# Projections of a hybrid decoder layer: one plain float32 matmul per weight block in place of three float32r passes

## Chip, core and metric

One core of one Trainium2 chip runs the program. The metric is the device time of one execution in microseconds (us), a median over runs. The core has TensorE (PE, whose weight loads are shown apart as PEld), VectorE (DVE), ScalarE (ACT), GpSimd (POOL) and SyncE (SP, which here only issues DMAs).

## What is computed

One inference step of one decoder layer on 320 tokens: 256 of a prompt and 8 sequences of 8 new tokens. Three residual parts follow each other, each behind an RMSNorm, all in float32:

```python
u, z, xbc, dt_raw, g_pool, g_ssm = jnp.split(h @ w_in, IN_SPLITS, axis=-1)
pooled, pool_new = _pool_mixer(u, pool_prev, pos, w_pool_group, pool_scale)
...
merged = jax.nn.sigmoid(g_pool) * (pooled @ w_pool_out) + jax.nn.sigmoid(g_ssm) * (y @ w_ssm_out)
x = x + merged @ w_out                                  # mixer: pooling and state-space branch
x = x + _cross_attn(_rmsnorm(x), mem_k, mem_v, w_q, w_o)  # 4 heads, 256 memory tokens
x = x + (jax.nn.silu(g) * v) @ w_down                   # g, v: causal conv of _rmsnorm(x) @ w_up
```

D_MODEL is 2048, the state-space branch is 4096 wide with 64 heads in 8 groups, the FFN is 5632 wide. The memory's keys and values (256 tokens by 2048) are projections too. Nearly all the arithmetic is such products of activations with weights that are read once.

## The kernel before

Activations lie with features on the partitions: 16 chunks of 128 features by 320 tokens. A projection (`dense`, line 92; `dense2`, line 104) makes a chunk of 128 outputs in a PSUM tile `acc` by adding up blocks: a block is 128 by 128 weights against 128 by 320 activations. The weights come in units of 128 by 1024 float32, 0.5 MB, eight blocks (`unit`, line 68), 785 in all.

A product is not one matmul. `unit` loads the unit into `raw` (line 73, SP's queue), casts it to float32r on ACT (`wh`, line 76) and has DVE subtract that from `raw` (`wl`, line 77): a high and a low part. The activations are split in the same way (`split`, line 120, and `split_gain`, line 124, with a gain in it): ACT makes the high part, DVE the low one (`a0h` and `a0l`, `a1h` and `a1l`, and so on). `mm3` (line 80) then issues three float32r matmuls per block: high by high (line 82), high weights by low activations (line 83), low weights by high activations (line 84). The memory's values have the tokens as the stationary side and 512 columns of weights as the moving one, three passes again (lines 229 to 231). The memory's keys go through `dense` with 256 tokens.

`raw` has 4 buffers, `wh` and `wl` 3 each. A scheduler orders each engine's instructions by priority, and `unit` runs at a priority AHEAD = 300 steps earlier than where it stands in the code, so that the loads and splits are queued ahead of the blocks that use them. SP's queue works in order: a load that waits for a buffer holds up what stands behind it, which also holds the loads of the states, of cached keys and values, of x and of constants.

The stages: `mem_and_norm` (line 198: memory values, the first norm, memory keys; `by_token` loads x and takes the memory's norm to tokens by two transposes of `rm`, line 288), `time_steps`, then eight groups of the state-space branch, whose scan (`ssd`, with `update`, line 611, the state updates by line 623) is woven between the projections; then the pooling branch, the output projection, cross-attention and the FFN. Some small products were plain float32 matmuls already: the sum of squares against ones in `rstd` (line 156), the attention's scores (line 882) and values (line 921), and the scan's products. `rstd` ends in a Newton step on DVE (lines 161 to 164), whose tile `newton` shares the tag `sq` and its two buffers with the squares of `square_into` (line 146).

Of the kernel before, what the change touches and what calls it, by code (L numbers as in the profile page):

```python
# [11 lines left out]
F32 = mybir.dt.float32  # L12
# [7 lines left out]
D = 2048  # L20
# [15 lines left out]
AHEAD = 300  # L36
SLABS = [(0, 12), (12, 12), (24, 12), (36, 8)]

# columns of the array of per-feature vectors
# [9 lines left out]
# columns of the array of constants  # L49
# [8 lines left out]
class Kernel:  # L58
# [9 lines left out]
    def unit(self, src):  # L68
        """Loads a [128, 1024] block of weights and splits it into high and low parts."""
        nc = self.nc  # L70
        with self.tc.high_priority(offset=self.ahead):
            raw = self.wraw.tile([128, 1024], F32, tag="raw", name="raw")
            nc.sync.dma_start(out=raw, in_=src)
            wh = self.wsp.tile([128, 1024], F32R, tag="wh", name="wh")
            wl = self.wsp.tile([128, 1024], F32R, tag="wl", name="wl")
            nc.scalar.copy(out=wh, in_=raw)  # L76
            nc.vector.tensor_tensor(out=wl, in0=raw, in1=wh.bitcast(F32), op=ALU.subtract)  # L77
        return wh, wl

    def mm3(self, out, wh, wl, xh, xl, first, last):  # L80
        nc = self.nc
# [10 lines left out]
    def dense(self, w, n, xh, xl, kc=KC, cols=128, t=T):  # L92
        """One chunk of outputs from kc chunks of inputs: a PSUM tile [cols, t]."""
        out = self.acc(t)[:cols]
        per = 1024 // cols
        for u in range((kc + per - 1) // per):
            wh, wl = self.unit(w[n, u] if cols == 128 else w)
            for j in range(min(per, kc - u * per)):
                k = u * per + j
                s = slice(j * cols, (j + 1) * cols)  # L100
                self.mm3(out, wh[:, s], wl[:, s], xh[:, k, :], xl[:, k, :], k == 0, k == kc - 1)
        return out

    def dense2(self, w, n2, k4s, xh, xl, k0=0):
        """Two chunks of outputs, units of two by four chunks: w[n2, u] holds [2, 4, 128]."""
        a = [self.acc(), self.acc()]
        for ui, u in enumerate(k4s):
            wh, wl = self.unit(w[n2, u])
            for o in range(2):
                for j in range(4):  # L110
                    s = slice((o * 4 + j) * 128, (o * 4 + j + 1) * 128)
                    k = k0 + ui * 4 + j
                    self.mm3(a[o], wh[:, s], wl[:, s], xh[:, k, :], xl[:, k, :],
                             ui == 0 and j == 0, ui == len(k4s) - 1 and j == 3)
        return a
# [4 lines left out]
    def split(self, hi, lo, src):  # L120
        self.nc.scalar.copy(out=hi, in_=src)  # L121
        self.nc.vector.tensor_tensor(out=lo, in0=src, in1=hi.bitcast(F32), op=ALU.subtract)  # L122
# [17 lines left out]
    def square_into(self, ssum, src, first, n):  # L140
        """Adds the squares of src to ssum."""
# [8 lines left out]
    def rstd(self, out, ssum, ones, n, more=()):  # L150
        """1 / sqrt(mean + eps) on all partitions, from sums of squares per partition."""
# [7 lines left out]
        # one Newton step: r * (1.5 - 0.5 * (mean + eps) * r * r)  # L159
# [32 lines left out]
    def acts0(self):  # L192
        return [self.a0.tile([128, KC, T], F32R, tag=t, name=t) for t in ("a0h", "a0l")]

    def acts1(self):
        return [self.a1.tile([128, KC, T], F32R, tag=t, name=t) for t in ("a1h", "a1l")]

    def mem_and_norm(self, p):
        """Keys and values of the memory; the first norm. Returns the jobs that remain."""
# [3 lines left out]
        self.xnh, self.xnl = self.acts0()  # L203
# [7 lines left out]
        mgh = p.tile([128, KC, MEM], F32R, name="mgh")  # L211
        mgl = p.tile([128, KC, MEM], F32R, name="mgl")
# [6 lines left out]
        def values(cb, before=lambda u: None):  # L219
            a = [self.acc(512), self.acc(512)]  # L220
            for u in range(8):
                before(u)
                wh, wl = self.unit(I["w_mem_v"][cb, u])
                for j in range(2):
                    k = 2 * u + j
                    s = slice(j * 512, j * 512 + 512)
                    for mc in range(2):
                        ms = slice(mc * 128, mc * 128 + 128)
                        nc.tensor.matmul(a[mc], lhsT=mgh[:, k, ms], rhs=wh[:, s], start=k == 0, stop=False)
                        nc.tensor.matmul(a[mc], lhsT=mgh[:, k, ms], rhs=wl[:, s], start=False, stop=False)  # L230
                        nc.tensor.matmul(a[mc], lhsT=mgl[:, k, ms], rhs=wh[:, s], start=False, stop=k == KC - 1)
# [10 lines left out]
        def norm_x():  # L242
            self.rstd(rx, sx, self.ones_d, T)
            for k in range(KC):
                xn = p.tile([128, T], F32, tag="xn", name="xn", bufs=2)
                nc.vector.scalar_tensor_tensor(out=xn, in0=x[:, k, :], scalar=self.vec(V_MIX + k), in1=rx,
                                               op0=ALU.mult, op1=ALU.mult)
                self.split(self.xnh[:, k, :], self.xnl[:, k, :], xn)
# [3 lines left out]
        def keys(n):  # L252
# [3 lines left out]
            a = self.dense(I["w_mem_k"], n, mgh, mgl, t=MEM)  # L256
# [5 lines left out]
        def split_mem(u):  # L262
# [4 lines left out]
            for k in (2 * u, 2 * u + 1):  # L267
                self.split_gain(mgh[:, k, :], mgl[:, k, :], m[:, k, :], self.gain_mkv[:, k:k + 1])
# [32 lines left out]
    def time_steps(self, s, p):  # L301
        """dt and the cumulated decays of all heads; their tables by token and by feature."""
# [9 lines left out]
        if True:  # L312
# [7 lines left out]
            a = self.dense(I["w_dt"], 0, self.xnh, self.xnl, cols=64)  # L320
# [5 lines left out]
            # log(1 + u) = 2 atanh(u / (2 + u))  # L326
# [85 lines left out]
    def xbc(self, s, g):  # L412
        """Projection, conv and SiLU of a group's B, C and x, features on partitions: six jobs."""
# [3 lines left out]
        def job(i):  # L417
# [8 lines left out]
            a = self.dense(I["w_xbc"], 6 * g + i, self.xnh, self.xnl)  # L426
# [24 lines left out]
    def ssd(self, s, g, r):  # L451
        """The scan of a group, in parts that go between other products."""
# [8 lines left out]
        def by_token():  # L461
# [12 lines left out]
            # B by token  # L474
# [5 lines left out]
            # C B, causal  # L480
# [10 lines left out]
            # decays between tokens, times C B  # L491
# [41 lines left out]
        def quads(q):  # L533
            """x and B of four batches by token, as high and low parts: rows [h l h l] and [h h l l]."""
# [77 lines left out]
        def update(i):  # L612
            """The states of two batches: rows of x against the batch's rows of B."""
# [32 lines left out]
    def gate(self, s, g, v, c):  # L646
        """y * silu(z) for one chunk."""
# [4 lines left out]
        a = self.dense(self.I["w_z"], 4 * g + c, self.xnh, self.xnl)  # L652
# [5 lines left out]
    def group_norm(self, s, g, v):  # L658
        """RMSNorm over the group, split."""
# [3 lines left out]
        yh = s.tile([128, 4, T], F32R, tag="yh", name="yh")  # L663
        yl = s.tile([128, 4, T], F32R, tag="yl", name="yl")
        for c in range(4):
            nc.vector.scalar_tensor_tensor(out=y[:, c], in0=y[:, c], scalar=self.vec(V_SN + 4 * g + c), in1=r,
                                           op0=ALU.mult, op1=ALU.mult)
            self.split(yh[:, c], yl[:, c], y[:, c])
        v["yhl"] = (yh, yl)

    def ssm_out(self, g, v, n2):
        nc = self.nc
        for o, a in enumerate(self.dense2(self.I["w_ssm_out"], n2, [g], *v["yhl"])):
# [6 lines left out]
    def gate_pool(self, s, c):  # L680
        """sigmoid of a chunk of the pooling branch's gates, kept in DRAM."""
        nc = self.nc
        a = self.dense(self.I["w_gp"], c, self.xnh, self.xnl)
# [4 lines left out]
    def mixer_ssd(self):  # L688
        self.gp_dram = self.dram.tile([128, KC, T], F32, name="gp_dram")
        with ExitStack() as st:  # L690
# [17 lines left out]
            for g in range(GROUPS):  # L708
# [8 lines left out]
                if prev is None:  # L717
                    # no earlier group to project: the same steps over fewer jobs
# [17 lines left out]
    def mixer_pool(self):  # L736
        nc, I, O = self.nc, self.I, self.O
        ph, pl = self.acts1()
        with ExitStack() as st:
# [8 lines left out]
            def window(k):  # L748
                dh = s.tile([128, 4, T], F32R, tag="dh", name="dh")
                dl = s.tile([128, 4, T], F32R, tag="dl", name="dl")  # L750
                w = 2 << k
                for i in range(4):
                    c = 4 * k + i
                    a = self.dense(I["w_u"], c, self.xnh, self.xnl)
# [14 lines left out]
                    df = s.tile([128, T], F32, tag="df", name="df", bufs=2)  # L769
# [5 lines left out]
                    self.split(dh[:, i], dl[:, i], df)  # L775
                return dh, dl

            def mix(k, d):
                for n2 in range(2):
                    for o, a in enumerate(self.dense2(I["w_pool_group"][k], n2, [0], *d)):  # L780
                        c = 4 * k + 2 * n2 + o
                        self.split_gain(ph[:, c], pl[:, c], a, self.vec(V_PS + c))
# [6 lines left out]
            for c in range(KC):  # L789
                a = self.dense(I["w_gs"], c, self.xnh, self.xnl)  # L790
# [8 lines left out]
            mh, ml = self.acts0()  # L799
# [420 lines left out]
```

## Time and profile before

| | us |
|---|---|
| median of 3 runs | 2975.48 (2974.54 to 2977.37) |
| profiled execution, span | 2977.2 |
| PE busy | 2930.6 (98%), 20082 instructions |
| PEld busy | 2841.3 (95%) |
| DVE busy | 1745.7 (59%) |
| ACT busy | 1311.4 (44%) |
| POOL busy | 512.6 (17%) |

Matmuls overlap in the profile: the duration of one runs from its start to the modelled end of its last output, so what a matmul costs in a stream is the distance from its start to the next start, not its duration. In a merged timeline row of n equal records that distance is the row's length less the last record's duration, by n - 1. Idle time of an engine is given with what ended it.

### The profile page before, as it was taken

The numbers are of one execution on the slowest core, as the hardware profiler recorded it, in microseconds if no ns is written. First come the engines' busy times: TensorE is split into PE (matmuls) and PEld (weight loads), VectorE is DVE, ScalarE is ACT, GpSimd is POOL, SyncE is SP. The second block draws the span as 40 slices with busy tenths as digits, with TensorE's granted clock in tenths as the row PEclk, the third lists the DMA queues.
The fourth block names the chain that finished last, engine by engine and source line by source line (L and its number), as shares of the span: only waits on it lengthen the run. The fifth ranks groups of instructions, "written<-read, shape, count | busy, mean of one in ns | idle before, by whom it ended". The sixth has DMA issues, their size and how long they took to land.

```text
span 2977.2 us, 49666 instructions
## 1 busy us (share of the span) xinstructions
PE 2930.6 (98%) x20082; PEld 2841.3 (95%) x20082; DVE 1745.7 (59%) x2442; ACT 1311.4 (44%) x1908; POOL 512.6 (17%) x624
## 2 busy tenths in 40 slices
PE   8999999999999999999999999999999999999997
PEld 6999899999999999999999998799999999999997
DVE  5667667677687565553355543356666646645644
ACT  6545555545545444443333433344444424433434
POOL 4014333243243220321111100010000000000002
PEclk9999999999999999999999999999999999999998
DMA  8775564555555645554556558744444444444443
GB/s 284 233 235 170 184 207 152 191 191 163 197 184 163 202 159 170 180 166 152 162 171 211 171 191 285 280 145 148 149 155 150 156 152 150 151 152 149 152 152 110
DMA packets 170150, 530.34 MB, mean 178 GB/s; under 512 B 20928, under 2 KB 47808, under 8 KB 165696
## 3 DMA queue, kind: packets, MB, share of 16 engines
q1 hardware_dynamic: 155360, 493.39, 51.1%
q10 hardware_dynamic: 14560, 33.78, 3.1%
q8 instruction: 157, 2.57, 0.4%
q14 instruction: 73, 0.60, 0.1%
HBM read 491.85 MB, written 35.25 MB: 177 GB/s over the span
## 4 chain that ended last, share of the span: by engine, by line
PE 86%; DMA 2%; DVE 1%; POOL 1%; issue 0%; ACT 0%; DVEq 0%; SPq 0%; ACTq 0%; POOLq 0%
PE acc L82 27%; PE acc L83 27%; PE acc L84 27%; DMA g<-la_dram 1%; PE misc L190 1%; DMA vc<-in_cache_v_dram 1%; PE misc L574 1%; DMA kc<-in_cache_k_dram 1%; PE misc L597 1%; PE misc L623 1%; PE misc L882 0%; PE misc L921 0%; PE misc L930 0%; DVE wl L77 0%; POOL g L495 0%
## 5 line engine op out<-in xcount | busy, mean ns | idle before, releaser
L77 DVE TENSOR_TENSOR wl<-raw,wh 128x1024 fp32r<-128x1024 f32 x785 | 1001.5, 1276 | 841.9 <-ACT wh L76 838.0
L76 ACT CAST wh<-raw 128x1024 fp32r<-128x1024 f32 x785 | 821.0, 1047 | 1235.4 <-PE acc L83 843.4
L82 PE MATMUL acc<-a0h,wh 128*128 128x320 f32 (+1 forms) x2960 | 922.1, 312 | 0.7 <-ACT a0h L121 0.7
L83 PE MATMUL acc<-a0l,wh 128*128 128x320 f32 (+1 forms) x2960 | 914.9, 309 | 0.4 <-DVE a0l L122 0.4
L84 PE MATMUL acc<-a0h,wl 128*128 128x320 f32 (+1 forms) x2960 | 914.8, 309 | 0.0
L82 PE MATMUL acc<-a1h,wh 128*128 128x320 f32 x1920 | 594.9, 310 | 0.0
L84 PE MATMUL acc<-a1h,wl 128*128 128x320 f32 x1920 | 593.4, 309 | 0.0
L83 PE MATMUL acc<-a1l,wh 128*128 128x320 f32 x1920 | 593.2, 309 | 0.0
L82 PEld LDWEIGHTS acc<-a0h,wh 128*128 128x128 f32 (+1 forms) x2960 | 555.8, 188 | 8.4 <-issue 3.6
L83 PEld LDWEIGHTS acc<-a0l,wh 128*128 128x128 f32 (+1 forms) x2960 | 556.1, 188 | 5.5 <-issue 3.2
L84 PEld LDWEIGHTS acc<-a0h,wl 128*128 128x128 f32 (+1 forms) x2960 | 555.9, 188 | 2.3 <-issue 2.1
L82 PEld LDWEIGHTS acc<-a1h,wh 128*128 128x128 f32 x1920 | 360.9, 188 | 6.0 <-issue 5.4
L83 PEld LDWEIGHTS acc<-a1l,wh 128*128 128x128 f32 x1920 | 361.0, 188 | 0.2
L84 PEld LDWEIGHTS acc<-a1h,wl 128*128 128x128 f32 x1920 | 360.9, 188 | 0.0
L82 PE MATMUL acc<-yh,wh 128*128 128x320 f32 x512 | 162.4, 317 | 0.0
L83 PE MATMUL acc<-yl,wh 128*128 128x320 f32 x512 | 159.7, 312 | 0.0
L84 PE MATMUL acc<-yh,wl 128*128 128x320 f32 x512 | 159.7, 312 | 0.0
L148 POOL TENSOR_TENSOR ssum<-ssum,sq 128x320 f32<-128x320 f32 x63 | 63.4, 1007 | 506.4 <-ACT sq L147 506.3
L1026 POOL COPY fnew<-fext 128x18 f32<-128x18 f32 x88 | 18.4, 209 | 546.1 <-DVE fext L1025 546.1
L438 DVE SCALAR_TENSOR_TENSOR ca<-ext,vecs,ca 128x344 f32<-128x344 f32 x144 | 99.2, 689 | 11.3 <-ACT ca L436 10.3
L82 PEld LDWEIGHTS acc<-yh,wh 128*128 128x128 f32 x512 | 97.7, 191 | 6.8 <-ACT sb L621 4.2
L1031 DVE SCALAR_TENSOR_TENSOR fca<-fext,vecs,fca 128x336 f32<-128x336 f32 x176 | 99.6, 566 | 3.1
(279 smaller groups left out, 3353.7 us busy)
## 6 DMA issues: line engine op xcount, KB each, us to landing
raw<-in_w_up_dram SPq DMA_DIRECT2D x176, 512.0 KB, 3.5
raw<-in_w_xbc_dram SPq DMA_DIRECT2D x96, 512.0 KB, 3.7
raw<-in_w_down_dram SPq DMA_DIRECT2D x88, 512.0 KB, 3.5
raw<-in_w_z_dram SPq DMA_DIRECT2D x64, 512.0 KB, 4.3
raw<-in_w_ssm_out_dram SPq DMA_DIRECT2D x64, 512.0 KB, 3.6
raw<-in_w_mem_v_dram SPq DMA_DIRECT2D x32, 512.0 KB, 4.9
raw<-in_w_mem_k_dram SPq DMA_DIRECT2D x32, 512.0 KB, 4.2
hin<-in_state_ssm_dram SPq DMA_DIRECT2D x32, 512.0 KB, 4.3
```

Of the source, the lines that this page charges most:

```text
L76: nc.scalar.copy(out=wh, in_=raw)
L77: nc.vector.tensor_tensor(out=wl, in0=raw, in1=wh.bitcast(F32), op=ALU.subtract)
L82: nc.tensor.matmul(out, lhsT=wh, rhs=xh, start=first, stop=False)
L83: nc.tensor.matmul(out, lhsT=wh, rhs=xl, start=False, stop=False)
L84: nc.tensor.matmul(out, lhsT=wl, rhs=xh, start=False, stop=last)
L148: nc.gpsimd.tensor_tensor(out=ssum, in0=ssum, in1=sq, op=ALU.add)
L190: self.nc.tensor.transpose(out, src, self.ident[:n, :n])
L438: nc.vector.scalar_tensor_tensor(out=ca[:, 0:344], in0=e[:, j:j + 344], scalar=self.vec(V_CW + 48 * j + c), in1=ca[:, 0:344], op0=ALU.mult ...
L574: nc.tensor.matmul(ps[64 * hh:64 * hh + 64, j * 128:j * 128 + n], lhsT=xd[j][:, h * 64:h * 64 + 64], rhs=gt[j][:, h, :n], start=True, stop ...
L597: nc.tensor.matmul(pq[32 * j:32 * j + 32, :], lhsT=Ct[:, SEQ + 8 * b:SEQ + 8 * b + 32], rhs=v["hin"][b // 2][:, b % 2, :], start=True, sto ...
L623: nc.tensor.matmul(ps, lhsT=sb, rhs=xr, start=True, stop=True)
L1031: nc.vector.scalar_tensor_tensor(out=ca[:, :336], in0=e[:, j:j + 336], scalar=self.vec(V_FW + 88 * j + c), in1=ca[:, :336], op0=ALU.mult, ...
```

## The change

Each projection block becomes one matmul with float32 operands. `unit` only loads; `split`, `split_gain` and `mm3` go; activations are kept once, in float32, written by the instruction that made them (or by `gained`, ACT alone). `raw` has 16 buffers and the pool of `wh` and `wl` is gone. The state-space branch's `y` gets two buffers, since the projection now reads it and not its split.

```diff
+WBUFS = 16
...
     def unit(self, src):
         with self.tc.high_priority(offset=self.ahead):
             raw = self.wraw.tile([128, 1024], F32, tag="raw", name="raw")
-            nc.sync.dma_start(out=raw, in_=src)
-            wh = self.wsp.tile([128, 1024], F32R, tag="wh", name="wh")
-            wl = self.wsp.tile([128, 1024], F32R, tag="wl", name="wl")
-            nc.scalar.copy(out=wh, in_=raw)
-            nc.vector.tensor_tensor(out=wl, in0=raw, in1=wh.bitcast(F32), op=ALU.subtract)
-        return wh, wl
+            self.nc.sync.dma_start(out=raw, in_=src)
+        return raw
-    def mm3(self, out, wh, wl, xh, xl, first, last):
-        nc.tensor.matmul(out, lhsT=wh, rhs=xh, start=first, stop=False)
-        nc.tensor.matmul(out, lhsT=wh, rhs=xl, start=False, stop=False)
-        nc.tensor.matmul(out, lhsT=wl, rhs=xh, start=False, stop=last)
+    def mm(self, out, w, x, first, last):
+        self.nc.tensor.matmul(out, lhsT=w, rhs=x, start=first, stop=last)
...
-    def split_gain(self, hi, lo, src, g):
-        self.nc.scalar.activation(out=hi, in_=src, func=AF.Copy, scale=g)
-        self.nc.vector.scalar_tensor_tensor(out=lo, in0=src, scalar=g, in1=hi.bitcast(F32),
-                                            op0=ALU.mult, op1=ALU.subtract)
+    def gained(self, out, src, g):
+        self.nc.scalar.activation(out=out, in_=src, func=AF.Copy, scale=g)
...
-        self.wraw = self.pool("wraw", 4)
-        self.wsp = self.pool("wsp", 3)
+        self.wraw = self.pool("wraw", WBUFS)
...
     def acts0(self):
-        return [self.a0.tile([128, KC, T], F32R, tag=t, name=t) for t in ("a0h", "a0l")]
+        return self.a0.tile([128, KC, T], F32, tag="a0", name="a0")
...
-            y = v["y"] = s.tile([128, 4, T], F32, tag="y", name="y")
+            y = v["y"] = s.tile([128, 4, T], F32, tag="y", name="y", bufs=2)
...
-                        self.split(oh[:, 4 * h + dc, :SEQ], ol[:, 4 * h + dc, :SEQ], ps)
+                        (nc.scalar.copy if dc % 2 else nc.vector.tensor_copy)(out=o_[:, 4 * h + dc, :SEQ], in_=ps)
```

The code loses its comments too, so line numbers move: line 82 to 84 become line 77, line 156 becomes 141, 190 becomes 174, 623 becomes 602, 586 becomes 565, 882 becomes 854.

On PE at the start of the program (memory values; `ssm` is the memory's sum of squares, `rm` its norm, `sx` the sum of squares of x), before, around the two transposes of `rm`:

```order
L229 MATMUL acc<-wh,mgh 128x512
L230 MATMUL acc<-wl,mgh 128x512
L231 MATMUL acc<-wh,mgl 128x512
L190 MATMUL misc<-cst,rm 128x128 x2
L229 MATMUL acc<-wh,mgh 128x512
```

and now, from the first matmul on:

```order
L77 MATMUL acc<-raw,mg 128x512 x36
L141 MATMUL misc<-ssm,ones_d 128x256
L77 MATMUL acc<-raw,mg 128x512 x27
L174 MATMUL misc<-cst,rm 128x128 x2
L77 MATMUL acc<-raw,mg 128x512 x33
L141 MATMUL misc<-sx,ones_d 128x320
L77 MATMUL acc<-raw,mg 128x512 x32
L77 MATMUL acc<-mg,raw 128x256 x128
```

The three passes have become one matmul, and the transposes stand behind 63 of them.

On SP's queue in the same place (`m` is the memory, `x_in` the input x), before:

```order
L266 DMA m<-in_mem_dram 128x1024
L73 DMA raw<-in_w_mem_v_dram 128x1024 x6
L274 DMA cst<-in_cst_dram 128x388
L73 DMA raw<-in_w_mem_v_dram 128x1024
L275 DMA vecs<-in_vecs_dram 128x752
L73 DMA raw<-in_w_mem_v_dram 128x1024
L277 DMA x_in<-in_x_dram 128x1280
```

and now:

```order
L245 DMA m<-in_mem_dram 128x1024
L73 DMA raw<-in_w_mem_v_dram 128x1024 x22
L253 DMA cst<-in_cst_dram 128x388
L254 DMA vecs<-in_vecs_dram 128x752
L73 DMA raw<-in_w_mem_v_dram 128x1024
L256 DMA x_in<-in_x_dram 128x1280
```

Six weight loads stand ahead of both pieces, so the first part of x is behind 14 loads before and behind 29 now.

On DVE in the first group of the state-space branch (`g` and `gs_` are the decays, `yo` the off-diagonal part, `hin` a state), before:

```order
L496 TENSOR_SCALAR g<-g 128x1024
L77 TENSOR_TENSOR wl<-raw,wh 128x1024
L496 TENSOR_SCALAR g<-g 128x1024
L586 TENSOR_TENSOR yo<-misc,el 128x4x128
L77 TENSOR_TENSOR wl<-raw,wh 128x1024
L608 TENSOR_TENSOR yo<-misc,el 128x4x32
```

and now:

```order
L475 TENSOR_SCALAR g<-g 128x1024 x2
L475 TENSOR_SCALAR gs__991<-gs__991 64x512
L565 TENSOR_TENSOR yo<-misc,el 128x4x128
L417 SCALAR_TENSOR_TENSOR ca<-ext_986,vecs,ca 128x344
L587 TENSOR_TENSOR yo<-misc,el 128x4x32
```

The weight splits are gone from between the steps, and the third minimum stands ahead of the first `yo`.

## Rows read from the trace of the kernel before

**Rows 1.** The page: busy time, granted clock, DMA total, chain by engine.
```profile
PE 2930.6 (98%) x20082; PEld 2841.3 (95%) x20082; DVE 1745.7 (59%) x2442; ACT 1311.4 (44%) x1908; POOL 512.6 (17%) x624
PEclk9999999999999999999999999999999999999998
DMA packets 170150, 530.34 MB, mean 178 GB/s; under 512 B 20928, under 2 KB 47808, under 8 KB 165696
...
PE 86%; DMA 2%; DVE 1%; POOL 1%; issue 0%; ACT 0%; DVEq 0%; SPq 0%; ACTq 0%; POOLq 0%
```

**Rows 2.** The page's groups, weight splits: count | busy us, mean ns | idle before, releaser.
```profile
L77 DVE TENSOR_TENSOR wl<-raw,wh 128x1024 fp32r<-128x1024 f32 x785 | 1001.5, 1276 | 841.9 <-ACT wh L76 838.0
L76 ACT CAST wh<-raw 128x1024 fp32r<-128x1024 f32 x785 | 821.0, 1047 | 1235.4 <-PE acc L83 843.4
```

**Rows 3.** Busy by stretch: length, PE, PEld, DVE, ACT, POOL (records), clock, DMA, GB/s.
```profile
2100.00:2400.00 300.00, 300.00 (x2047) 300.00 (x2046) 188.65 (x308) 126.32 (x164) 19.27 (x78) 1.00 0.48 154
```

**Rows 4.** Scores: timeline of PE (start, length), and the line's records (ns min/median/max).
```profile
1759.61 3.18 PE L882 MATMUL misc<-kt,qt 128*128 128x256 f32 x14
...
L882 PE MATMUL misc<-kt,qt x64: 378/379/382, 1759.6 to 1899.9; 128*128 128x256 f32 x64
```

**Rows 5.** Sum of squares against ones: timeline of PE, and the line's records.
```profile
344.96 0.70 PE L156 MATMUL misc<-ssum,ones_g 128*128 128x320 f32 x2
...
L156 PE MATMUL misc<-ssum,ones_g x16: 431/432/432, 345.0 to 1152.3; 128*128 128x320 f32 x16
```

**Rows 6.** Block counts: line 82 over the span (PE, PEld), keys, values by form.
```profile
0.00:2977.20 2977.20, 1870.37 (x6032) 1134.62 (x6032) 0.99 0.55 178
...
L82 PE MATMUL acc<-mgh,wh 128*128 128x256 f32 x256 | 72.4, 283 | 0.0
...
L229 PE MATMUL acc<-wh,mgh 128*128 128x512 f32 x128 | 52.3, 410 | 8.1 <-ACT wh L76 7.3 <-ACT v L237 0.8
```

**Rows 7.** Busy by stretch, in the memory's keys.
```profile
180.00:200.00 20.00, 20.00 (x169) 20.00 (x168) 11.83 (x20) 8.15 (x10) 0.98 (x4) 1.00 0.75 261
```

**Rows 8.** Timeline of PE in the memory's values: first and fifteenth of a run.
```profile
99.66 0.39 PE L231 MATMUL acc<-wh,mgl 128*128 128x512 f32 x1
...
102.94 0.39 PE L230 MATMUL acc<-wl,mgh 128*128 128x512 f32 x1
```

**Rows 9.** Waits of PE: who waited for whom, us in total, times, longest.
```profile
PE misc L623 <- DVE yo L586: 10.9, 6, 3.8
PE acc L229 <- ACT wh L76: 7.3, 1, 7.3
PE misc L623 <- ACT sb L621: 4.0, 1, 4.0
```

**Rows 10.** Timelines of DVE and of PE behind PE's longest interior stall.
```profile
300.86 1.51 DVE L496 TENSOR_SCALAR g<-g 128x1024 f32<-128x1024 f32 x1 [2.62 <-POOL g L495]
...
302.89 1.21 DVE L77 TENSOR_TENSOR wl<-raw,wh 128x1024 fp32r<-128x1024 f32 x1
...
306.68 0.47 PE L82 MATMUL acc<-a0h,wh 128*128 128x320 f32 x1
306.95 0.47 PE L83 MATMUL acc<-a0l,wh 128*128 128x320 f32 x1
```

**Rows 11.** The start: two stretches, x's first square, the norm's end, early passes.
```profile
0.00:60.00 60.00, 51.81 (x207) 40.21 (x208) 37.05 (x40) 42.47 (x74) 30.50 (x35) 1.00 0.77 269
60.00:80.00 20.00, 19.88 (x86) 15.67 (x85) 9.90 (x9) 9.20 (x12) 3.34 (x2) 1.00 0.94 325
...
L144 ACT ACTIVATE sx<-x_in x1: 455/455/455, 40.4 to 40.4; 128x320 f32<-128x320 f32 x1
...
L164 DVE TENSOR_TENSOR rm<-rm,newton x1: 426/426/426, 45.6 to 45.6; 128x256 f32<-128x256 f32 x1
...
10.84 0.63 PE L230 MATMUL acc<-wl,mgh 128*128 128x512 f32 x1
11.26 0.63 PE L231 MATMUL acc<-wh,mgl 128*128 128x512 f32 x1
```

More of the change, by code (lines that the diff above doesn't have):

```diff
@@ L90, in misc, with dense @@
         return self.psm.tile([128, 512], F32, tag="misc", name="misc")
-    def dense(self, w, n, xh, xl, kc=KC, cols=128, t=T):
+    def dense(self, w, n, x, kc=KC, cols=128, t=T):
         out = self.acc(t)[:cols]
@@ L192, in acts0 @@
     def acts0(self):
-        return [self.a0.tile([128, KC, T], F32R, tag=t, name=t) for t in ("a0h", "a0l")]
+        return self.a0.tile([128, KC, T], F32, tag="a0", name="a0")
     def acts1(self):
-        return [self.a1.tile([128, KC, T], F32R, tag=t, name=t) for t in ("a1h", "a1l")]
+        return self.a1.tile([128, KC, T], F32, tag="a1", name="a1")
     def mem_and_norm(self, p):
@@ L228, in values @@
                         ms = slice(mc * 128, mc * 128 + 128)
-                        nc.tensor.matmul(a[mc], lhsT=mgh[:, k, ms], rhs=wh[:, s], start=k == 0, stop=False)
-                        nc.tensor.matmul(a[mc], lhsT=mgh[:, k, ms], rhs=wl[:, s], start=False, stop=False)
-                        nc.tensor.matmul(a[mc], lhsT=mgl[:, k, ms], rhs=wh[:, s], start=False, stop=k == KC - 1)
+                        self.mm(a[mc], mg[:, k, ms], wt[:, s], k == 0, k == KC - 1)
             return a
@@ L244, in norm_x @@
             for k in range(KC):
-                xn = p.tile([128, T], F32, tag="xn", name="xn", bufs=2)
-                nc.vector.scalar_tensor_tensor(out=xn, in0=x[:, k, :], scalar=self.vec(V_MIX + k), in1=rx,
+                nc.vector.scalar_tensor_tensor(out=self.xn[:, k, :], in0=x[:, k, :], scalar=self.vec(V_MIX + k), in1=rx,
                                                op0=ALU.mult, op1=ALU.mult)
-                self.split(self.xnh[:, k, :], self.xnl[:, k, :], xn)
         kts = {}
@@ L425, in job @@
                 nc.gpsimd.memset(r["C"][:, T:], 0.0)
-            a = self.dense(I["w_xbc"], 6 * g + i, self.xnh, self.xnl)
+            a = self.dense(I["w_xbc"], 6 * g + i, self.xn)
             e = self.ext[self.ei % 3]
@@ L651, in gate @@
         y = v["y"]
-        a = self.dense(self.I["w_z"], 4 * g + c, self.xnh, self.xnl)
+        a = self.dense(self.I["w_z"], 4 * g + c, self.xn)
         z = s.tile([128, T], F32, tag="z", name="z", bufs=1)
@@ L667, in group_norm @@
                                            op0=ALU.mult, op1=ALU.mult)
-            self.split(yh[:, c], yl[:, c], y[:, c])
-        v["yhl"] = (yh, yl)
     def ssm_out(self, g, v, n2):
         nc = self.nc
-        for o, a in enumerate(self.dense2(self.I["w_ssm_out"], n2, [g], *v["yhl"])):
+        for o, a in enumerate(self.dense2(self.I["w_ssm_out"], n2, [g], v["y"])):
             dst = self.accs[:, 2 * n2 + o]
@@ L682, in gate_pool @@
         nc = self.nc
-        a = self.dense(self.I["w_gp"], c, self.xnh, self.xnl)
+        a = self.dense(self.I["w_gp"], c, self.xn)
         t = s.tile([128, T], F32, tag="z", name="gp", bufs=1)
@@ L748, in window @@
             def window(k):
-                dh = s.tile([128, 4, T], F32R, tag="dh", name="dh")
-                dl = s.tile([128, 4, T], F32R, tag="dl", name="dl")
+                d_ = s.tile([128, 4, T], F32, tag="d_", name="d_", bufs=2)
                 w = 2 << k
@@ L753, in window @@
                     c = 4 * k + i
-                    a = self.dense(I["w_u"], c, self.xnh, self.xnl)
+                    a = self.dense(I["w_u"], c, self.xn)
                     e = exts[c % 2]
@@ L774, in window @@
                                                    scalar=1.0 / w, in1=es[:, :, 15:], op0=ALU.mult, op1=ALU.subtract)
[L775 to L776 removed]
+                return d_
             def mix(k, d):
                 for n2 in range(2):
[L780 removed]
+                    for o, a in enumerate(self.dense2(I["w_pool_group"][k], n2, [0], d)):
                         c = 4 * k + 2 * n2 + o
[L782 removed]
+                        self.gained(ph[:, c], a, self.vec(V_PS + c))
             d = window(3)
@@ L789, in mixer_pool @@
             for c in range(KC):
-                a = self.dense(I["w_gs"], c, self.xnh, self.xnl)
+                a = self.dense(I["w_gs"], c, self.xn)
                 t = s.tile([128, T], F32, tag="z", name="gs", bufs=1)
@@ L803, in mixer_pool @@
                     nc.sync.dma_start(out=sg, in_=self.gp_dram[:, c:c + 4])
-                a = self.dense(I["w_pool_out"], c, ph, pl)
+                a = self.dense(I["w_pool_out"], c, ph)
                 t = sg[:, c % 4]
                 nc.vector.tensor_tensor(out=t, in0=t, in1=a, op=ALU.mult)
-                nc.gpsimd.tensor_tensor(out=t, in0=t, in1=self.accs[:, c], op=ALU.add)
-                self.split(mh[:, c], ml[:, c], t)
-        return mh, ml
+                nc.gpsimd.tensor_tensor(out=m[:, c], in0=t, in1=self.accs[:, c], op=ALU.add)
+        return m
     def residual(self, c, a, gain, hl):
@@ L815, in residual, with mixer_out @@
         if gain is not None:
-            self.split_gain(hl[0][:, c], hl[1][:, c], self.x[:, c], self.vec(gain + c))
+            self.gained(hl[:, c], self.x[:, c], self.vec(gain + c))
         self.sum_square(c, self.x[:, c])
-    def mixer_out(self, mh, ml):
+    def mixer_out(self, m):
         nc, I = self.nc, self.I
@@ L826, in mixer_out @@
         for c in range(KC):
-            self.residual(c, self.dense(I["w_out"], c, mh, ml), V_MQ, hl)
+            self.residual(c, self.dense(I["w_out"], c, m), V_MQ, hl)
         return hl
@@ L833, in next_rstd, with attention @@
         return r
-    def attention(self, xh, xl):
+    def attention(self, xg):
         nc, I, O = self.nc, self.I, self.O
         sc = 1.0 / math.sqrt(HD)
-        oh, ol = self.acts0()
+        o_ = self.acts0()
         with ExitStack() as st:
@@ L940, in values_out @@
                     cs = slice(SEQ + 32 * q, SEQ + 32 * q + 32)
-                    self.split(oh[:, 4 * h:4 * h + 4, cs].rearrange("p c (b t) -> p c b t", b=4),
-                               ol[:, 4 * h:4 * h + 4, cs].rearrange("p c (b t) -> p c b t", b=4), src)
+                    nc.vector.tensor_copy(out=o_[:, 4 * h:4 * h + 4, cs].rearrange("p c (b t) -> p c b t", b=4), in_=src)
                 return [
@@ L1008, in up @@
                 else:
-                    hl = [s.tile([128, 12, T], F32R, tag=t, name=t) for t in ("fh", "fl")]
+                    hl = s.tile([128, 12, T], F32, tag="fh", name="fh")
                 prev = s.tile([128, 2, 12, NB, 2], F32, tag="fprev", name="fprev", bufs=1)
@@ L1016, in up @@
                         c = v * FC + i0 + i
-                        a = self.dense(I["w_up"], c, xh, xl)
+                        a = self.dense(I["w_up"], c, xg)
                         if not rxs:
@@ L1035, in up @@
                         parts.append(ca)
-                    ac = s.tile([128, T], F32, tag="ac", name="ac", bufs=2)
+                    ac = hl[:, i]
                     g_, v_ = parts
@@ L1051, in down @@
                 for c2 in range(KC // 2):
-                    for o, a in enumerate(self.dense2(I["w_down"], c2, range(i0 // 4, (i0 + n) // 4), *hl)):
+                    for o, a in enumerate(self.dense2(I["w_down"], c2, range(i0 // 4, (i0 + n) // 4), hl)):
                         c = 2 * c2 + o
@@ L1083, in run @@
             m = self.mixer_pool()
-            hl = self.mixer_out(*m)
-            hl = self.attention(*hl)
-            self.ffn(*hl)
+            hl = self.mixer_out(m)
+            hl = self.attention(hl)
+            self.ffn(hl)
             self.final()
```

56 lines of the change are left out of this document (23 added, 33 removed).

## The prediction, made before the changed kernel ran

> **What bounds the kernel now.** I read the page's first part, then the chain that ended last: PE is busy 2930.6 of 2977.2 us and has 86% of the chain, and its weight loads are 95% busy [rows 1]. A busy PE is not yet a PE at its limit, so the next view is one dense stretch. From 2100 to 2400 us (the up-projection) PE has no idle time, the clock is at 1.00, and 2047 records touch the 300 us; two of them cross its edges, so one pass starts every 300/2045 = 0.1467 us [rows 3]. A block (128 by 128 weights against 320 tokens) takes three such passes: 0.440 us. The splits that feed those passes look costly (1001.5 us on DVE, 821.0 on ACT), but the idle time in front of them is 842 and 1235 us, and most of it waits for ACT's half or for PE to free a buffer [rows 2]: both engines run behind PE, not ahead of it. DMA moves 530 MB, 178 GB/s on the mean [rows 1], where it carried 269 in the first 60 us [rows 11]; at that rate the bytes need 1970 us. So PE's passes are the bound, and the question is what a plain float32 matmul costs on PE against three passes of 0.1467 us.
>
> **The price of a plain block.** The trace has plain float32 matmuls already, in the attention and the norms. The scores of a head run just behind a dense stretch: at 1759.61 fourteen records of 256 columns take 3.18 us, the last of them 0.379, so they start (3.18 - 0.379)/13 = 0.2155 us apart [rows 4]. That is two records per matmul: four heads times 2 times 4 is 32 matmuls in the program, and the view of that line counts 64 [rows 4]. So 256 columns cost 0.431 us, at full clock, each with new weights. The other width that is there is the one needed: the sum of squares against ones, 320 columns, two records in 0.70 us with a last one of 0.432, so 0.268 apart [rows 5]; 0.2155 x 320/256 gives 0.2694. I take 0.269, 0.538 us a block (bounds 0.536 and 0.540). Three passes cost 0.440, so **each block becomes 0.098 us dearer**.
>
> **Part by part.**
> Blocks of 320 tokens: line 82 issues the first pass of each block and counts 6032, of which 256 are the memory keys', so 5776 are left [rows 6]. 5776 x 0.098 = +566 us (bounds 554 and 578). All of it lies on PE, nothing covers it.
> Memory keys, 256 blocks of 256 tokens [rows 6]: from 180 to 200 us 169 records touch 20 us, 167 starts, 0.1198 apart [rows 7]; three are 0.359, plain is 0.431, so 256 x 0.072 = +18 us.
> Memory values, 128 blocks of 512 columns [rows 6]: 14 starts from 99.66 to 102.94 us are 0.2343 apart [rows 8], three are 0.703; plain by columns is 4 x 0.2155 = 0.862; 128 x 0.159 = +20 us.
> The weight splits leave DVE and ACT (1001.5 and 821.0 us [rows 2]), and so do the splits of the activations. What PE gets from that is only idle time that it has now. Its list of waits is short: 10.9 us for DVE and 4.0 us for ACT in front of the state updates (line 623), 7.3 at the start [rows 9]; what is left is a few microseconds of loads in the attention. The one at 300 us shows the mechanism: DVE's scaling of the off-diagonal part (line 586) stands in its queue behind a minimum that waited 2.62 us for POOL, and behind that a weight split of 1.21 us stands ahead of the next step [rows 10]; the state update itself waits for those steps to free its PSUM buffer. The split goes; POOL's part stays, and in the new order the third minimum of the group stands ahead of line 586's step too, but PE gives both more time, since eight blocks last 4.3 us where they lasted 3.5. After the stall PE's passes start 0.27 apart for a while [rows 10], half the usual rate, so a stall costs more than its idle time. I take **-15 us**; bounds 0 and -30 (all of line 623's 14.9, the other interior waits, and the slow passes behind each).
> The start: PE's first matmul waits 7.3 us for the cast of the first weight block [rows 9]; without the cast -1 us (0 to -2). The number of weight buffers rises from 4 raw and 3 split to 16, and a load is put on SP's queue 300 steps early in both, which is now more blocks, as a block has fewer steps. So SP's queue runs further ahead, and what is behind 29 weight loads in it waits for PE to finish 13 blocks. The input x is there: in the order before it follows 14 loads, now 29. 29 loads of 0.52 MB, the memory tokens (2.1 MB) and constants are 18 MB, at 269 GB/s 67 us, at 325, the most that one stretch of 20 us reached [rows 11], 55 us. Who waits for x: DVE's Newton step for the memory's norm writes a buffer of the squares' tag, so it waits for POOL to add the first squares of x (the tag has two buffers), and behind it the two transposes of that norm on PE. PE comes to them after 63 plain matmuls: 6.3 + 63 x 0.862 + some 3 for its slow first microseconds (passes 0.43 apart as late as 11 us, where 0.234 is usual [rows 8, 11]) = 63 us. In the trace the norm is done 5.6 us after x's first square starts (40.4 to 46.0 [rows 11]), so it would be ready between 60 and 72: a new stall of 0 to 10 us, I take **+5**.
> Later SP loads with the same risk (states, cached keys) wait for buffers of their own that are freed many blocks before the weights behind them are needed, 16 blocks being 69 us of PE work; I cost them at nothing, and at 5 us if I am wrong. Weights are no new bound: 0.5 MB per 4.3 us is 122 GB/s. The gain on the mixer's y (two buffers instead of one plus its split) is freed DVE and ACT time off the path.
>
> **Sum**: 2977.2 + 566 + 18 + 20 - 15 - 1 + 5 = 3570 us for the profiled execution. The runs of before had a median 1.7 us under the profiled span, so 3569; I say 3570. Low end: 2977 + 554 + 37 - 30 - 2 = 3536; high end: 2977 + 578 + 39 + 10 + 5 = 3609.
>
> **Rivals.** (1) *Faster: the second record costs nothing of its own.* If a block were worth one record of 0.269, PE would lose 5776 x 0.171 = 988 us, and with DMA at 1970 us the kernel would take about 2000. The kernel is faster than before from the point where a block costs less than 0.440, that is a record under 0.22. Against it: records of 256 columns stand 0.2155 apart and those of 320 columns 0.268, in proportion to columns, and each matmul has two [rows 4, 5]; nor can the freed DVE and ACT pay, since PE is idle only 46.6 us in all [rows 1]. The Trainium skill, Perfetto Trace Analysis, section Engine Utilization, gives the array's output rate as divided by 2 for FP32_LOW_HIGH; taken as the price of a whole float32 matmul, that is this rival. The trace agrees with it for one record only (0.2155 us for 256 columns is half of 2.4 GHz), and every matmul has two of them. 2%.
> (2) *Dearer in a long stream.* The passes of today start 0.1467 apart where 320 columns at 2.4 GHz are 0.133, 10% more; the plain rows show 1% more (0.269 to 0.267). The plain ones are short runs; if hundreds in a row pay the 10% too, a block costs 0.587, and 6160 blocks add 0.05 us each: about 3870. Fourteen in a row, with new weights for each matmul, show none of it [rows 4]. 4%.
> (3) *The clock.* If a mostly plain stream were granted 1.2 GHz for part of the time, each per cent of the time costs 36 us. The fourteen plain records at 1759 us run at the full rate, right behind three-pass work; no long plain stretch is there to look at. 3%, at 3650 and above.
> (4) *The freed engines hide more than I think, or the start's stall is longer*: inside the bounds above.
> That the change doesn't do what it says is out: the order on PE has one matmul per block.
>
> **How the numbers follow.** The forecast's case has 90%, rivals 1 to 3 have 2, 4 and 3%, and 1% is left for no change. The range 3535 to 3610 is that of the forecast's own bounds; the other cases lie outside it and hold 10%. Faster by over 0.2% 2%, within 0.2% (what a measurement of this kernel can tell from no change, some 6 us) 1%, slower 97%.
>
> **What would show it.** In the profile after, a dense stretch at full clock has records 0.269 apart, 1115 in 300 us. PE's records number 20082 less 18480 passes plus 12320, 13922. DVE is busy under 750 us and ACT under 500, PE over 98%; the chain is again PE's. Around 63 us PE waits a few microseconds for the transposes of the memory's norm, and line 623's successor waits in one group at most. A spacing under 0.22 us, a spacing near 0.29, or a clock row below 9 would each make the forecast wrong, by the rival named.

## The result and the profile after

The changed kernel takes 3560.3 us (median of 4 runs, 3559.49 to 3561.03), the one before 2975.0 beside it: a ratio of 1.196, 95% interval 1.195 to 1.198. The forecast was 3570 in a range from 3535 to 3610. The profiled execution has a span of 3559.2 us against 2977.2.

From the page of the kernel after, as in [rows 1]: the busy times (share of the span, instructions), the granted clock and the total of the DMA:

```profile
PE 3528.7 (99%) x13922; PEld 2463.6 (69%) x13922; DVE 700.9 (20%) x1461; ACT 491.0 (14%) x989; POOL 393.3 (11%) x624
PEclk9999999999999999999999999999999999999999
DMA packets 170077, 529.36 MB, mean 149 GB/s; under 512 B 20928, under 2 KB 47808, under 8 KB 165696
```

DVE lost 1045 us of work and ACT 820, and PE still has almost no idle time: 30.5 us of the span, where it had 46.6. PE's records fell from 20082 to 13922, the number that two records per plain matmul make. What one of them costs is read in a stretch without idle time, as in [rows 3]. Busy time by stretch of the kernel after (length, then PE, PEld, DVE, ACT, POOL with their records, clock, DMA share, GB/s), first the start, then the up-projection:

```profile
0.00:60.00 60.00, 54.06 (x122) 24.08 (x123) 0.00 (x0) 18.28 (x41) 11.87 (x23) 1.00 0.87 321
2500.00:2800.00 300.00, 300.00 (x1116) 211.74 (x1115) 68.09 (x173) 31.35 (x52) 16.93 (x69) 1.00 0.40 125
```

1116 records touch the 300 us and two of them began before it: 300/1114 = 0.2693 us a record, 0.539 us a block, where three passes took 0.440. The weight loads are busy for 212 of the 300 us where they were busy all the time [rows 3], so it is not their rate that sets the price of a block.

PE's waits in the kernel after, which answer to [rows 9] (who waited for whom: us in total, times, longest):

```profile
PE acc L77 <- DMA raw<-in_w_mem_v_dram: 5.9, 1, 5.9
PE misc L602 <- ACT sb L600: 5.1, 6, 3.2
PE misc L876 <- DMA kc<-in_cache_k_dram: 1.7, 1, 1.7
PE misc L174 <- DVE rm L149: 0.5, 1, 0.5
```

The start is the load itself now, 5.9 us where it was load and cast, 7.3. The state updates (line 602, line 623 before) wait 5.1 us in place of 14.9. The transposes of the memory's norm (line 174) wait half a microsecond, where I had put 5 us.

### The profile page after: what moved, and what is told of

Its sections match the earlier page's. It is cut to its first block, busy times and chain, and to the rows that moved or that the text cites. A ratio compares the mean times of both kernels' runs of the same rounds, so it can differ in the third digit from the quotient of the medians.

```text
span 3559.2 us, 34307 instructions
## 1 busy us (share of the span) xinstructions
PE 3528.7 (99%) x13922; PEld 2463.6 (69%) x13922; DVE 700.9 (20%) x1461; ACT 491.0 (14%) x989; POOL 393.3 (11%) x624
## 5 line engine op out<-in xcount | busy, mean ns | idle before, releaser
L77 PE MATMUL acc<-a,raw 128*128 128x320 f32 (+1 forms) x9760 | 2647.3, 433 | 0.4 <-DVE a L913 0.4
L77 PEld LDWEIGHTS acc<-a,raw 128*128 128x128 f32 (+1 forms) x9760 | 1848.7, 190 | 781.2 <-issue 17.1
L77 PE MATMUL acc<-y,raw 128*128 128x320 f32 x1024 | 284.1, 434 | 0.0
L77 PEld LDWEIGHTS acc<-y,raw 128*128 128x128 f32 x1024 | 192.2, 190 | 81.8 <-DVE accs L653 5.0
L77 PE MATMUL acc<-fh,raw 128*128 128x320 f32 x640 | 172.6, 432 | 0.0
L1000 ACT ACTIVATE fca<-fext,vecs 128x336 f32<-128x336 f32 x88 | 58.7, 667 | 820.2 <-DVE fext L997 820.2
L77 PEld LDWEIGHTS acc<-fh,raw 128*128 128x128 f32 x640 | 121.6, 190 | 50.7
L77 PE MATMUL acc<-raw,mg 128*128 128x512 f32 x256 | 113.0, 602 | 5.9 <-DMA raw<-in_w_mem_v_dram 5.9
L77 PE MATMUL acc<-mg,raw 128*128 128x256 f32 x512 | 110.9, 379 | 0.0
L77 PEld LDWEIGHTS acc<-mg,raw 128*128 128x128 f32 x512 | 97.2, 190 | 14.1 <-issue 1.0
L594 POOL TENSOR_TENSOR hin<-hin,dec 128x1024 f32<-128x1024 f32 x32 | 63.5, 2005 | 77.3 <-PE misc L576 77.3
```

Source lines behind the costliest of these rows:

```text
L77: self.nc.tensor.matmul(out, lhsT=w, rhs=x, start=first, stop=last)
L594: nc.gpsimd.tensor_tensor(out=t.rearrange("p b (h d) -> p b h d", h=8), in0=t.rearrange("p b (h d) -> p b h d", h=8), in1=bcast(self.dec[: ...
L1000: nc.scalar.activation(out=ca[:, :336], in_=e[:, :336], func=AF.Identity, scale=self.vec(V_FW + c), bias=self.vec(V_FB + c))
```

## The experiments

Each is timed beside the kernel before on its own chip. That had a median of 2979.4 us for the runs in the FFN alone, without the low part, with 4 buffers and with two passes, and of 2980.2 for the three others.

**One part alone: plain blocks in the FFN.** The kernel before, with the projections of the FFN as plain blocks of float32 weights and activations, and all others in three passes.

```diff
-                        a = self.dense(I["w_up"], c, xh, xl)
+                        a = self.dense_plain(I["w_up"], c, xf)
...
-                    for o, a in enumerate(self.dense2(I["w_down"], c2, range(i0 // 4, (i0 + n) // 4), *hl)):
+                    for o, a in enumerate(self.dense2_plain(I["w_down"], c2, range(i0 // 4, (i0 + n) // 4), hl)):
```

> The kernel before with plain float32 blocks in the FFN alone (176 + 88 units, 2112 blocks), its weights and activations not split, 4 raw buffers as before. If each block is dearer by 0.098 us wherever it stands, +207 us: 3182 us (3170 to 3190). If the loss of the whole change comes from something that grows with the whole program (queue order, buffers, clock), clearly less or more than 207.

Measured: 3185.6 us, ratio 1.0695 (1.0679 to 1.0711), 206 us over the kernel before beside it. 206/2112 = 0.0976 us a block, and 0.098 was the estimate. Its dense stretch, in the FFN:

```profile
2500.00:2800.00 300.00, 300.00 (x1116) 211.77 (x1115) 54.66 (x135) 21.79 (x36) 11.83 (x48) 1.00 0.39 124
```

The same 1116 records as in the kernel after. The loss comes with the blocks and needs nothing of the change outside the FFN: 2112 of the 6160 blocks are 34%, and 206 of 585 us are 35%.

**The splits without the passes.** The kernel before, where DVE no longer makes the weights' low part; the third pass takes the high part a second time.

```diff
-            wl = self.wsp.tile([128, 1024], F32R, tag="wl", name="wl")
...
-            nc.vector.tensor_tensor(out=wl, in0=raw, in1=wh.bitcast(F32), op=ALU.subtract)
-        return wh, wl
+        return wh, wh
```

> The kernel before, without DVE's low part of the weights: the third pass of each block uses the high part again, so one correction term is missing from the products. PE's work is the same, DVE loses some 1000 us. If PE's passes are the bound, only idle time in front of PE can go: about 2960 us (2945 to 2977), PE at 0.1467 us a pass in dense stretches. If the weight splits hold PE up in a way that its idle time doesn't show, the kernel gains 100 us or more.

Measured: 2976.7 us (10 runs), ratio 0.9991 (0.998 to 1.0001): no change that this measurement can tell. The page, and PE's waits for line 621, which is line 623 of the kernel before:

```profile
PE 2929.8 (98%) x20082; PEld 2842.2 (95%) x20082; DVE 778.6 (26%) x1657; ACT 1317.3 (44%) x1908; POOL 384.5 (13%) x624
...
PE misc L621 <- ACT sb L619: 13.5, 6, 3.3
PE misc L621 <- DVE yo L584: 3.8, 1, 3.8
```

DVE did 967 us less and PE got nothing for it. The stall in front of the state updates is no shorter, 17.3 us against 14.9, but it is another one: it was put down to DVE in the kernel before (10.9 of 14.9 us) and is put down to ACT here. DVE's step for `yo` ends 0.6 us behind the minimum in the second to seventh group, where it ended 1.7 us behind it, and PE waits for ACT's `sb` instead; a cast of weights is among the work that ACT does just ahead of it, and the order on PE is another too (mostly twelve blocks between the second and the third update, where there were eight). So taking DVE's split away moved the wait and did not shorten it.

**The splits beside plain blocks.** The changed kernel with both splits of the weights kept as dead work, and 8 weight buffers.

```diff
-WBUFS = 16
+WBUFS = 8
...
+            self.nc.scalar.copy(out=wh, in_=raw)
+            self.nc.vector.tensor_tensor(out=wl, in0=raw, in1=wh.bitcast(F32), op=ALU.subtract)
         return raw
...
```

> The changed kernel with the weight splits kept as dead work: every unit is still cast on ACT and subtracted on DVE, and nothing reads the two parts; 8 weight buffers. If PE's interior idle time shrank with the change (22.5 to 7.7 us) because its blocks last longer, it stays near 8 and the time near 3560 us (3555 to 3570). If it shrank because DVE and ACT are rid of the splits, it goes back to some 20 us, and the time to 3575 or more.

Measured: 3559.4 us. The page, and the waits that answer to the ones above:

```profile
PE 3528.7 (99%) x13922; PEld 2464.0 (69%) x13922; DVE 1633.8 (46%) x2246; ACT 1273.5 (36%) x1768; POOL 488.0 (14%) x624
...
PE acc L81 <- ACT sq L136: 6.1, 1, 6.1
PE misc L607 <- ACT sb L605: 4.2, 2, 3.4
PE misc L881 <- DMA kc<-in_cache_k_dram: 1.4, 1, 1.4
```

With 933 us more on DVE and 783 more on ACT than the kernel after, PE's busy time is the same to a tenth of a microsecond and the stall is 4.2 us, not 15. Together the two runs show that the work of the weight splits, as a load on DVE and ACT, costs PE nothing. They do not show why the stall shrank, because the dead split does not stand where the live one did. In the kernel before, a split stands between the minimum and the step for `yo` in each of the second to seventh groups; in this run it does so in none of them. The third group in both, first before:

```profile
512.02 0.69 DVE L496 TENSOR_SCALAR g<-g 128x1024 f32<-128x1024 f32 x1 [3.88 <-POOL g L495]
512.63 1.22 DVE L77 TENSOR_TENSOR wl<-raw,wh 128x1024 fp32r<-128x1024 f32 x1
513.76 0.68 DVE L586 TENSOR_TENSOR yo<-misc,el 128x512 f32<-128x512 f32 x1
514.60 0.69 PE L623 MATMUL misc<-xr,sb 128*128 128x512 f32 x1 [2.26 <-DVE yo L586]
...
601.64 0.69 DVE L480 TENSOR_SCALAR g<-g 128x1024 f32<-128x1024 f32 x1 [2.89 <-POOL g L479]
602.25 0.48 DVE L658 TENSOR_TENSOR accs<-accs,acc 128x320 f32<-128x320 f32 x1
602.65 0.68 DVE L570 TENSOR_TENSOR yo<-misc,el 128x512 f32<-128x512 f32 x1
```

**The weight buffers.** The changed kernel with 4 buffers.

```diff
-WBUFS = 16
+WBUFS = 4
```

> The changed kernel with 4 weight buffers in place of 16. Eight plain blocks last 4.3 us and a load lands in 3.5, so three loads ahead are enough in the dense stages: 3560 us, within 10. If the depth of 16 is what keeps PE fed through the states' and cached keys' loads, 30 us or more are lost, in the state-space groups and the attention.

Measured: 3559.2 us, ratio 1.1948 (1.1931 to 1.1966), a microsecond from 16 buffers. PE's waits are 6.0 us at the start, 4.3 for the state updates, 1.5 for cached keys, and the half microsecond of the norm's transposes is not in the list any more. Between 4 and 16 buffers the depth of the prefetch is worth nothing here.

**Fewer passes.** The kernel before with two passes; the one of high weights by low activations is left out, so that part of each product is missing. In the memory's values it is the one of low weights by high activations.

```diff
-        nc.tensor.matmul(out, lhsT=wh, rhs=xl, start=False, stop=False)
...
-                        nc.tensor.matmul(a[mc], lhsT=mgh[:, k, ms], rhs=wl[:, s], start=False, stop=False)
```

> The kernel before with two passes per block in place of three: the pass of high weights by low activations is left out. If a pass costs PE its 0.1467 us and nothing else is near, 5776 x 0.1467 + 256 x 0.120 + 128 x 0.234 = 908 us go: 2067 us. DVE's 1746 us of work and DMA's 1970 us (530 MB at 269 GB/s) come near then, so 2067 to 2200; over 2200 a split or a load is the next bound. If PE's time does not follow its passes, less than 450 us go.

Measured: 2281.9 us, ratio 0.7658 (0.7647 to 0.767). 698 us went, and not 908: this is the outcome over 2200 us. Two stretches of it, one in the FFN and one in the state-space groups, and three of PE's waits:

```profile
1800.00:2000.00 200.00, 200.00 (x1366) 200.00 (x1365) 168.35 (x274) 120.15 (x149) 26.55 (x62) 1.00 0.74 226
200.00:400.00 200.00, 179.36 (x1191) 164.34 (x1190) 166.96 (x207) 141.35 (x243) 89.92 (x85) 0.96 0.73 235
...
PE acc L83 <- DVE wl L77: 19.9, 15, 4.5
PE misc L572 <- ACT s L555: 18.9, 6, 3.6
PE misc L189 <- DVE rm L163: 16.4, 1, 16.4
```

Where PE is dense it is still the bound, at 0.1466 us a pass (200/1364). Elsewhere the chains that three passes covered come up: PE is idle for 186 us of the span, in many waits for DVE, ACT and loads, and the mean granted clock is 0.966. The third pass had hidden most of that: the kernel before was idle for 46.6 us at a mean clock of 0.995.

**What sets 0.1467 us.** The kernel before with bfloat16 parts in place of float32r ones, three passes as before, the activations' parts likewise; each operand is kept to about 16 bits, so low bits of the products are lost.

```diff
-            wh = self.wsp.tile([128, 1024], F32R, tag="wh", name="wh")
-            wl = self.wsp.tile([128, 1024], F32R, tag="wl", name="wl")
+            wh = self.wsp.tile([128, 1024], BF16, tag="wh", name="wh")
+            wl = self.wsp.tile([128, 1024], BF16, tag="wl", name="wl")
...
```

> The kernel before with bfloat16 parts in place of float32r parts (weights and activations each a high and a low bfloat16; three passes as before), so 16 bits of each operand count. If a float32r pass starts 0.1467 us after the last one because of its format, where 320 columns at 2.4 GHz are 0.1333, a bfloat16 pass starts about 0.136 after: -189 us for the 5776 blocks, -15 for keys and values, 2771 us (2750 to 2790). If the loading of new weights for each pass sets it, no change: 2975 us.

Measured: 2804.5 us, ratio 0.9415 (0.9397 to 0.9434). The stretch of [rows 3], the first and the seventh of a run of passes in the memory's values, and the largest of PE's interior waits:

```profile
2100.00:2400.00 300.00, 300.00 (x2211) 216.12 (x2209) 190.81 (x296) 128.01 (x161) 16.67 (x68) 1.00 0.52 163
...
98.78 0.38 PE L232 MATMUL acc<-wh,mgl 128*128 128x512 bf16 x1
...
100.07 0.38 PE L232 MATMUL acc<-wh,mgl 128*128 128x512 bf16 x1
...
PE misc L624 <- DVE yo L587: 15.8, 6, 3.2
PE misc L905 <- DMA kc<-in_cache_k_dram: 5.9, 4, 2.5
PE misc L624 <- ACT sb L622: 4.5, 1, 4.5
```

The starts in the 300 us are 0.1358 apart on the mean, where 320 columns at 2.4 GHz take 0.1333. So the pass is as cheap as was expected of it, and the excess of 10% came with the float32r operands. In this stretch the weight loads fell too, from all of it to 216 us. The memory's values tell the two apart: there the float32r passes of 512 columns start 0.2343 apart [rows 8], 10% over the 0.2133 of 2.4 GHz, with the weight loads busy for only 15.7 of 20 us [rows 11], and the bfloat16 ones (100.07 - 98.78)/6 = 0.215. So the rate of the weight loads does not make the excess there. Which of the two operands' formats does stays open. Of the 204 us expected, some 175 came; PE's idle time grew from 46.6 to 71.1 us, which fits blocks that last less long and cover less, and is not tested further.

**One pass.** The changed kernel with float32r operands: weights cast on ACT, activations rounded by the instruction that writes them. Both operands keep their high part alone, so the products lose all low parts.

```diff
+            wh = self.wsp.tile([128, 1024], F32R, tag="wh", name="wh")
+            self.nc.scalar.copy(out=wh, in_=raw)
+        return wh
...
-        return self.a0.tile([128, KC, T], F32, tag="a0", name="a0")
+        return self.a0.tile([128, KC, T], F32R, tag="a0", name="a0")
...
```

> The changed kernel with one float32r pass per block: weights cast on ACT, activations rounded by the instruction that writes them, no low parts at all, 10 raw and 4 cast buffers; both operands keep only their high part. PE's passes come to 5776 x 0.1467 + 256 x 0.120 + 128 x 0.234 = 908 us, some 1100 with the rest, so PE is no longer the bound. DMA is: 530 MB at 269 to 325 GB/s, 1970 to 1630 us. Expected 1900 us (1700 to 2050), with PE waiting for weights in the dense stages. If something that the passes cover now comes up (the scan's chain, ACT's casts), over 2100.

Measured: 1745.3 us, ratio 0.5862 (0.5846 to 0.5879), the fastest of all. From its page, the whole span as one stretch (as in [rows 3]), and its largest waits of PE:

```profile
PE 1307.0 (75%) x7762; PEld 1139.5 (65%) x7762; DVE 693.5 (40%) x1461; ACT 1249.5 (72%) x1793; POOL 406.6 (23%) x624
GB/s 378 282 378 367 266 298 202 324 210 286 244 252 312 237 331 245 286 298 240 253 355 320 324 333 366 262 347 335 308 238 287 374 315 359 387 320 335 334 383 161
DMA packets 170038, 528.64 MB, mean 303 GB/s; under 512 B 20928, under 2 KB 47808, under 8 KB 165696
...
0.00:1742.60 1742.60, 1307.01 (x7762) 1139.53 (x7762) 693.54 (x1461) 1249.46 (x1793) 406.61 (x624) 0.86 0.82 303
...
PE acc L79 <- DVE fext L1001: 66.5, 9, 15.2
PE acc L79 <- ACT z L636: 42.6, 20, 4.0
PE acc L79 <- ACT wh L75: 35.8, 33, 7.3
```

It is faster than the 1970 us that I had called the need of its bytes: 303 GB/s on the mean, up to 387 in a slice. No single engine is busy all the time: the DMA engines for 82% of the span on the mean, PE for 75%, ACT for 72%. PE waits for others to empty its accumulators, for casts and for loads in turn. Its busy time is 1307 us where some 1100 were expected, with a mean granted clock of 0.86.

## Why the prediction was right

**The price of a block.** This was the argument, and it held to the third digit: 0.268 us a record was read off a pair of records [rows 5] and 0.2694 by columns from fourteen [rows 4], 0.2693 is what a thousand in a row take. 5776 blocks make 5776 x (0.5386 - 0.440) = 570 us where 566 were put down. The fourteen stood in the same company as the later ones: full clock, new weights for each matmul, directly behind dense work. That this is why so few were enough is likely and was not tested.

**The sum, term by term.** The starts in the two traces show where PE's time went. In this table each matmul record is charged with the distance to the next start, without idle time (us):

| | before | after | change | forecast |
|---|---|---|---|---|
| blocks of 320 tokens | 2557.1 | 3119.3 | +562.2 | +566 |
| memory keys | 92.2 | 110.8 | +18.6 | +18 |
| memory values | 93.9 | 112.5 | +18.6 | +20 |
| all other matmuls | 187.3 | 186.1 | -1.2 | 0 |
| idle at the start | 7.3 | 5.9 | -1.3 | -1 |
| idle between matmuls, without x's stall | 22.5 | 7.2 | -15.3 | -15 |
| x's stall | 0 | 0.5 | +0.5 | +5 |
| behind the last matmul | 16.9 | 16.9 | 0 | 0 |

One thing is allowed for in it. A float32r record right behind a plain float32 one is shown as starting 0.03 us after it, so that the plain one's time falls into the next distance: behind the pair of [rows 5], whose second record starts at 345.23, a pass is shown at 345.26 and the next one at 345.65. Such a plain record (61 before, 17 after) is charged with the distance that is usual for its width.

The changes make the 582 us by which the span grew; the forecast was 593. Nearly half of the difference is x's stall. The blocks came 4 us under their term and 8 under the price of dense ones. Some 4 of the 8 are the clock: in the kernel before, 42 passes behind the three longest stalls of the state updates ran at a granted clock of 0.50 (1.2 GHz) and took 11.5 us, where 42 x 0.1467 is 6.2, and in the kernel after only 4 records did. The longest of these stretches, before:

```profile
303.20:309.80 6.60, 5.53 (x20) 4.92 (x20) 5.88 (x11) 1.85 (x5) 0.44 (x2) 0.50 0.48 171
```

The other matmuls, which the prediction didn't name, stayed as they were.

**Idle time.** -15 us came out of the sum for stalls, and so many went between PE's matmuls, 9.8 of them in front of the state updates. (The prediction's term was also to hold the slow passes behind the stalls; those are the 4 us above.) Of the two reasons that it gave, one can be measured: PE gives the chain more time. In the second to seventh group eight blocks stand between the second and the third state update, before and after. In the eighth, where nothing waits, they hold the third update back by 0.55 us more than before. The waits of the six groups fell by 1.5 us each, from 1.8 to 0.3. The rest is a chain that ends sooner: `yo` was done 6.1 us behind the group's products with the state `s` (line 585) on the mean, and is done 3.8 us behind them now; what PE still waits for there is ACT's `sb`. The split of 1.2 us that had stood in that chain is gone, as the prediction said, but the minimum ahead of it also ends 1.5 us sooner, and no run takes these apart. So how much the split's going brought stays open, and that the term came out to the number is in part luck. The forecast that line 623's successor would wait in one group at most was wrong: it waits in six, in one of them for 3.2 us. That the chain of waits would again be PE's can't be read: in the page of the kernel after that view shows only the last steps, on DVE.

**x behind 29 loads.** The term that was furthest off. 18 MB at 269 to 325 GB/s were to bring x's part at 55 to 67 us, and the memory's norm at 60 to 72. The queue behaves as described (x is issued at 53.7 us, its first square starts at 58.7, the Newton step waits for it), but the first 60 us carried 321 GB/s, near the upper of the two rates. (The 13 and 16 "blocks" of PE's work in that paragraph of the prediction are units of weights.) The rows of the tile of `rm` in the kernel after (min/median/max ns, first and last start in us):

```profile
L174 PE MATMUL misc<-cst,rm x2: 272/300/328, 63.2 to 63.4; 128*128 128x128 f32 x2
...
L149 DVE TENSOR_TENSOR rm<-rm,newton x1: 424/424/424, 62.8 to 62.8; 128x256 f32<-128x256 f32 x1
```

The norm was done at 63.2 us, PE came to it at 62.8, and the cost was 0.5 us where +5 had been put down.

**The rivals.** That the second record costs nothing is out: 1116 records in 300 us, two per block. The row that spoke against it before spoke rightly, and the reading of the Trainium skill's division by 2 (Perfetto Trace Analysis, Engine Utilization) as the price of a whole float32 matmul would have been wrong by a factor of two; as the price of one of its records it agrees with 0.2693 us. That a long stream of plain records pays the 10% of the float32r passes is out as well, and the bfloat16 run fits that: there most of the 10% is gone. The clock stayed up: the mean granted clock was 0.998 after and 0.995 before. The one number of the rivals that fell is the DMA floor of 1970 us. It took the rate of the first 60 us as the most that the queues can carry, though a row beside it had 325 GB/s [rows 11]; the run with one pass moved nearly the same bytes in 1743 us. It carried no weight in the forecast, but it would have in one on fewer passes.

## What to carry to other kernels

Price an operation by start-to-start distances of the same operation in the trace, at the width that the change will use, and multiply; a dozen records behind dense work gave the price of a plain block to a tenth of a per cent. Relieving two engines of half their work brought nothing here while a third one was the bound, and keeping that work as dead work is a way to test it. But such a run tests the load alone: look where the scheduler has put the dead work before reading from it what a chain of waits was worth. A rate seen under a kernel that doesn't ask for more is no ceiling, so a floor that is made from it is none either.

## What was not expected of the hardware

A float32r pass of 320 columns starts 0.1467 us after the last one, and a bfloat16 pass 0.1358, at the same granted clock; a plain float32 matmul comes, as forecast, as two records of 0.2693, four times 320 columns at 2.4 GHz (0.533) and 1% more. So three float32r passes cost 0.440 us, three of bfloat16 0.407 and one of plain float32 0.539. One core's DMA carried 387 GB/s over a fortieth of the span when something asked for it, where the kernel before never had more than 285 in such a slice.
